# The second block of v columns in a gMLP layer: eight block products against seven, on one Trainium2 core

## The chip, the cores and the metric

The kernel runs on one core of one Trainium2 chip. The metric is the device time of one execution in microseconds (us). TensorE (PE) multiplies matrices, its weight loads are listed apart as PEld; VectorE (DVE) and ScalarE (ACT) do element-wise work, GpSimd (POOL) a few fills, and SyncE (SP) issues nearly all the transfers from memory.

## The reference, cut to what matters

The model is a trunk of two layers on 512 tokens of width 1024: attention, a dense SwiGLU, then a gMLP ("token mixing") and a second SwiGLU. Each sub-layer's output is normalised, gated and added to x, and x is normalised, scaled and shifted into the next sub-layer's input h. The change is in the gMLP:

```python
def token_mixing_mixer(h, w_in, ln_g, w_s, b_s, w_out):
    uv = jax.nn.gelu(h @ w_in)            # (512, 1024) @ (1024, 2048)
    u, v = jnp.split(uv, 2, axis=-1)      # 1024 columns each
    v = layer_norm(v, ln_g)               # over the 1024 columns of v
    ...                                   # chunks of 128 tokens, 8 groups of 128 columns
    sv = jnp.einsum('gts,bnsgc->bntgc', ws, v) + b_s.T[None, None, :, :, None]
    return (u * sv.reshape(B, S, D)) @ w_out
```

## The kernel before, in words

**Numbers in two parts.** Every operand of a matrix product is kept as a high and a low part in a reduced float32 (`F32R`). `split` writes the high part with ACT (a copy) and the low part with DVE (the difference). `mm3` then makes one product with three matmuls: high x high, high x low, low x high. A tile of 128x1024 numbers that comes from memory ("raw") therefore costs one ACT copy ("wh") and one DVE subtraction ("wl") before TensorE can use it.

**Weights.** `stream` is the list of all weight tiles in order of use. `wget(key, look)` hands out the next one and emits the loads and splits of up to `look` tiles beyond it. A raw tile lies in the pool `wraw`, which has two buffers; a split pair lies in `wpool` and `wpool2`, together six buffers. `s4` is a pool of 28 slots of 4 KB for everything else. Loads go through SP's queue in one order.

**Who sets the order.** The program is handed to a scheduler that fixes the order of instructions on each engine when the kernel is built, by program order and by its own estimate of when operands and buffers are there. Each engine then works its list from front to back and waits where something is late. In some stages the kernel chains the order by hand (`pe["chain"]`, `dve.chain`); not in the gMLP.

**The boundary in front of the gMLP.** `out_proj` ends the first SwiGLU; for each of four token tiles `tt` of 128 tokens, `boundary` normalises, adds to x, normalises again, has TensorE transpose the result ("tp") and splits it into `hT` (the input, features on the partitions). While the last two tiles pass through, three jobs fill TensorE: `v_first` twice (first 512 columns of v, token tiles 0 and 1) and `u_first` (the first 128 columns of u, tokens 0 to 255).

**The gMLP.** `gmlp` does, in order: the first 512 columns of v for token tiles 2 and 3 (48 matmuls of 128x512); the rest of u's first block (24 of 128x256); the second 512 columns of v for all four token tiles (96 of 128x512); gelu and `bn_stats`; then u's blocks 1 to 7 (`u_unit`), between which the normalised v is mixed (`mix`, "sv"). For v, the stationary operand is a 128x128 piece of `hT` and the moving one a row of 512 weight columns. Weight tiles of v are `("win_v", half, j)`, each with 256 of the 1024 input features, four for a half.

**In the background.** `bg.step(n)` advances the preparation of the next boundary's scale and shift ("A", "B"): each step loads 512 KB of modulation weights ("rawada") and adds a multiple of an earlier one to a sum on DVE (`scalar_tensor_tensor`, "B<-rawada,sc,B"). Its buffers are two.

**Seven products, elsewhere in this kernel.** Both SwiGLUs already compute a 2x2 block product by seven half-size products instead of eight (`Ffn.seven`): the weights are cut in four blocks B11, B12, B21, B22, of which sums T1 to T4 are made; of the activations the sums "1" to "4" are needed, which `boundary` makes with `sums` when it is given a dictionary `S`. For the first two token tiles it keeps an unsplit copy ("c"); for each of the other two, `sums` makes four DVE additions ("fs") and four splits ("Sh", "Sl"). At the boundary in front of the gMLP, `S` was None.

**Offsets.** `wtile` places a pair at an offset inside its buffer: 16 by default, `SHORT` (29 and 61 in turn) for the weights of matmuls that are 256 wide, 0 for the seven-product blocks of the last down projection.

Of the kernel before, what the change touches and what calls it, by code (L numbers as in the profile page):

```python
# [33 lines left out]
def trunk(ctx: ExitStack, tc: tile.TileContext, A: dict, out: bass.AP):  # L34
# [109 lines left out]
    def wload():  # L144

        src, a, b, key = stream[len(raws)]
        if src is None:
            raws.append(block_loads(key[1]))
            return
        raw = wraw.tile([P, a, b], F32, tag="raw", name=nm("raw"))  # L150
        load(raw[:], src)
        raws.append(raw)

    def wemit():
        n = len(got)
        src, a, b, key = stream[n]
        if len(raws) == n:
            wload()
        if src is None:
            if not first_blocks or n > first_blocks[-1] + KF:  # L160
                first_blocks.append(n)
            for _ in blocks(*next_raws(n)):
                pass
            return
        raw = raws[n]
        if key[0] == "wdn" and key[2] in SEVEN[key[1]]:
            got.append(down_blocks(raw))
            return
        h, l = wtile(a, b, SHORT if key[0] in ("wgu", "win_u") else 16)
        if key[0] == "wqk" and key[1]:  # L170

            act.activation(h[:], raw[:], AF.Copy)
            nc.vector.tensor_tensor(l[:], raw[:], h[:].bitcast(F32), ALU.subtract)
            if len(raws) == n + 1 and stream[n + 1][3][0] == "wqk":
                wload()
        else:
            high = act.activation(h[:], raw[:], AF.Copy)
            last_low[0] = nc.vector.tensor_tensor(l[:], raw[:], h[:].bitcast(F32), ALU.subtract)  # L178
# [17 lines left out]
    def block_loads(idx):  # L196

        x = wraw.tile([P, KD, P], F32, tag="raw", name=nm("rawx"))
        y = fwork["raw"].tile([P, KD, P], F32, tag="raw2", name=nm("rawy"))
        load(x[:], A["wx"][idx])
        load(y[:], A["wy"][idx])
        return x, y

    def next_raws(n):

# [115 lines left out]
    for l in range(2):  # L324
        for f in range(NH):
            wadd("wgu", 8, P, l, f, 0)
            wadd("wgu", 8, P, l, f, 1)
        for f in range(NH, KF):
            stream.append((None, 0, 0, ("blocks", (l, f - NH))))
        if l == 1:  # L330
            for q in range(2):
                for p in PAIRS[q]:
                    wadd("wdn", 4, 256, q, p)
        if l == 0:
            for f in range(KF):
                wadd("wdown", 1, D, f)
            for j in range(4):
                wadd("win_v", 2, 512, 0, j)
            wadd("win_u", 8, P, 0)
            for j in range(4):  # L340
                wadd("win_v", 2, 512, 1, j)
            for m in range(1, KD):
                wadd("win_u", 8, P, m)
            for k in range(KD):
                wadd("wout", 1, D, k)
# [1105 lines left out]
        return lambda: [v_gelu(v0["b"], tt, 0) for tt in range(2) if 3 in js]  # L1451

    def u_first(hT):
        v0["u"] = wget(("win_u", 0), 1)
        return u_unit(hT, 0, 0, 256, v0["u"])

    def gmlp(bg, hT, nhT, nS, nxt):
# [5 lines left out]
        u_unit(hT, 0, 256, 256, v0["u"])()  # L1463
        for tt in (2, 3):
            v_gelu(vb, tt, 0)
        vb = [bank("v") for _ in range(NT)]
        for k in range(4):
            if k % 2 == 0:
                wv = wget(("win_v", 1, k // 2))
            for tt in range(NT):  # L1470
                v_mm(hT, vb, tt, k, wv)
            bg.step(STEPS)
        wsr = wraw.tile([P, KD, P], F32, tag="raw", name="wsr")
        load(wsr[:], A["ws"])
        nc.gpsimd.memset(wsr[0:64, :, 64:P], 0.0)
# [2 lines left out]
            split(w[:, :, 0:P], w[:, :, P:], wsr[:, 4 * i : 4 * i + 4, :])  # L1478
        bsb = slot(F32, "bsb", KD, P)
        load(bsb[:].rearrange("p a b -> p (a b)"), A["bs"].to_broadcast([P, D]))  # L1480
        tail = [wget(("win_v", 1, j)) for j in (2, 3)]
        st = small.tile([P, NT, 2, 6], F32, tag="bns", bufs=1, name=nm("bns"))
        mv = small.tile([P, NT, 2], F32, tag="mv", bufs=1, name=nm("mv"))
        for tt in range(NT):
            for k in range(4, KD):
                v_mm(hT, vb, tt, k, tail[k // 2 - 2])
            v_gelu(vb, tt, 1)
            for hf in range(2):
                dve.bn_stats(st[:, tt, hf, :], vt[tt][:, 0, hf * 512 : (hf + 1) * 512])
            dve.bn_aggr(mv[:, tt, :], st[:, tt, :, :])  # L1490
# [69 lines left out]


    hT1, hT2, hT3 = {}, {}, {}
    S1, S3 = {}, {}
# [5 lines left out]
    bg2 = Bg("A2", "B2", lag=1, gap=3)  # L1569
    f0.run(  # L1570
        Bg("G1", slots=1), Bg("A1", "B1", "G2", slots=3, lag=2, flat=True), bg2, 2, hT2,
        [lambda: v_first(hT2, (0, 1)), lambda: v_first(hT2, (2, 3)), lambda: u_first(hT2)],
    )
    gmlp(bg2, hT2, hT3, S3, f1.first())
    f1.last(Bg("G3", slots=1))
# [2 lines left out]
def _layout(i):  # L1578

    f = np.ascontiguousarray  # L1580

    def fout(w):
        m = w.shape[1] // P
        return w.reshape(KD, P, m, P).transpose(2, 1, 0, 3)

    def blocks(a, b):

        return (
            np.concatenate([a[:, :, :4], b[:, :, 4:]], 2),
            np.concatenate([a[:, :, 4:], b[:, :, :4]], 2),  # L1590
        )
# [12 lines left out]
    wqkv = i["sb_w_qkv"][0]  # L1604
    a["wqk"] = np.stack([fout(wqkv[:, :D]), fout(wqkv[:, D : 2 * D])], 1)
    a["wv"] = vhalf(wqkv[:, 2 * D :])
    a["wo"] = slabs(i["sb_w_o"][0])
    gu = [(fout(i["ffn_w_gate"][l]), fout(i["ffn_w_up"][l])) for l in range(2)]
    a["wgu"] = np.stack([np.stack([g[:3], u[:3]], 1) for g, u in gu])
    a["wx"], a["wy"] = [np.stack(t) for t in zip(*[blocks(g[3:], u[3:]) for g, u in gu])]  # L1610
    a["wdown"] = slabs(i["ffn_w_down"][0])

    w = i["ffn_w_down"][1].reshape(NF, 2, P, 2, 2, 256).transpose(4, 0, 2, 1, 3, 5)
    w = w.reshape(2, NF, P, 4, 256).copy()
    for q in range(2):
# [4 lines left out]
    a["win_v"] = vhalf(i["tm_w_in"][0][:, D:])  # L1620
    a["wout"] = slabs(i["tm_w_out"][0])
# [55 lines left out]
```

## Time and profile before

| | before |
|---|---|
| median of 3 runs | 1104.61 us (1103.84 to 1106.79) |
| span of the profiled execution | 1104.6 us, which is the time of the median run to the digits shown |
| PE busy | 1085.9 us (98%), 7404 matmuls |
| PEld busy | 979.0 us (89%) |
| DVE busy | 945.9 us (86%) |
| ACT busy | 594.2 us (54%) |
| second half of v on TensorE | 649.81 to 671.59 us, 96 matmuls |
| u's blocks 1 to 4 on TensorE, behind it | 671.59 to 693.92 us, 192 matmuls |

A matmul's time in the list is longer than the step from one matmul to the next, since matmuls overlap in the array; what counts is the step, that is the difference of two starts. Times in the timeline are microseconds from the span's start.

### The profile page before, as it was taken

The page shows a single profiled execution, that of the slowest core. Times are in us where ns is not written, and L with a number is a line of the kernel's source. Part 1 is how long each engine was busy: PE and PEld are TensorE (multiplying, and loading weights), DVE is VectorE, ACT ScalarE, POOL GpSimd, SP SyncE. Part 2 cuts the span into 40 slices and gives each one's busy share as a digit, 9 for nine tenths or more (in the row PEclk, how much of TensorE's full clock was granted, in tenths as well). Part 3 has the DMA queues.
Part 4 walks back from the last instruction along what each step waited for, and adds up shares of the span by engine and source line. Part 5 has one row for each costly group of instructions (what it writes and reads, how often), then busy time and mean ns, then how long its engine had stood idle before and what let it go on. Part 6 is the DMA issues. An engine that isn't in the chain of part 4 may idle for free.

```text
span 1104.6 us, 18512 instructions
## 1 busy us (share of the span) xinstructions
PE 1085.9 (98%) x7404; PEld 979.0 (89%) x7404; DVE 945.9 (86%) x1248; ACT 594.2 (54%) x982; POOL 29.5 (3%) x53
## 2 busy tenths in 40 slices
PE   6999999999999999999999999999999999999997
PEld 4787788788999999998888889988999999989996
DVE  4988999966989999989866967668979999899997
ACT  6554665665655555554243626426555555565662
POOL 0020100000000000000000000001000000000000
PEclk9999999999999999999999999999999999999999
DMA  8976434304433434359757465334334343333252
GB/s 302 370 226 217 142 116 133 125 11 152 157 112 131 162 119 146 132 197 351 272 191 256 144 205 196 96 116 155 128 117 155 128 159 102 110 115 96 77 187 81
DMA packets 51355, 176.38 MB, mean 160 GB/s; under 512 B 6074, under 2 KB 9146, under 8 KB 51268
## 3 DMA queue, kind: packets, MB, share of 16 engines
q1 hardware_dynamic: 48708, 166.81, 44.6%
q0 software_dynamic: 2560, 8.39, 2.1%
q8 instruction: 58, 0.95, 0.3%
q14 instruction: 29, 0.24, 0.1%
HBM read 164.69 MB, written 8.39 MB: 157 GB/s over the span
## 4 chain that ended last, share of the span: by engine, by line
PE 90%; DVE 4%; DMA 2%; ACT 2%; issue 1%; SPq 0%; DVEq 0%; ACTq 0%
PE r L109 32%; PE y L109 18%; PE pqk L109 7%; PE gu L109 6%; PE v L109 5%; PE X L109 4%; PE u L109 4%; PE Y L109 3%; PE av L109 2%; PE z L109 2%; PE tw L117 1%; PE tp L117 1%; PE Z L109 1%; PE W L109 1%; PE ab L109 1%
## 5 line engine op out<-in xcount | busy, mean ns | idle before, releaser
L87 ACT ACTIVATE wh<-raw 128x1024 fp32r<-128x1024 f32 (+1 forms) x112 | 115.7, 1038 | 130.5 <-PE y L109 39.4
L109 PE MATMUL r<-Sh,wh 128*128 128x256 f32 x608 | 168.1, 276 | 0.5 <-ACT e L87 0.5
L109 PE MATMUL r<-Sh,wl 128*128 128x256 f32 x608 | 167.9, 276 | 0.0
L109 PE MATMUL r<-Sl,wh 128*128 128x256 f32 x608 | 167.9, 276 | 0.0
L109 PE MATMUL y<-wh,as 128*128 128x512 f32 x480 | 149.9, 390 | 0.0
L178 DVE TENSOR_TENSOR wl<-raw,wh 128x1024 fp32r<-128x1024 f32 x87 | 105.8, 1222 | 48.2 <-ACT wh L87 47.6
L109 PEld LDWEIGHTS r<-Sh,wh 128*128 128x128 f32 x608 | 114.1, 188 | 1.0 <-ACT e L87 0.9
L109 PEld LDWEIGHTS r<-Sl,wh 128*128 128x128 f32 x608 | 114.1, 188 | 0.1
L109 PEld LDWEIGHTS r<-Sh,wl 128*128 128x128 f32 x608 | 114.1, 188 | 0.0
L109 PEld LDWEIGHTS y<-wh,as 128*128 128x128 f32 x480 | 90.0, 188 | 18.6
L71 DVE TENSOR_TENSOR wl<-f,wh 128x1024 fp32r<-128x1024 f32 x87 | 103.2, 1220 | 0.0
L87 ACT ACTIVATE wh<-f 128x1024 fp32r<-128x1024 f32 x87 | 91.8, 1055 | 15.3 <-DVE f L71 11.6
L87 ACT ACTIVATE e<-r 128x256 f32<-128x256 f32 x114 | 43.7, 385 | 101.8 <-PE r L109 100.8
L109 PE MATMUL y<-wl,as 128*128 128x512 f32 x240 | 93.7, 391 | 0.0
L109 PE MATMUL r<-hTh,wh 128*128 128x256 f32 x304 | 84.2, 277 | 0.2 <-DVE gu L71 0.2
L109 PE MATMUL r<-hTl,wh 128*128 128x256 f32 x304 | 84.0, 276 | 0.0
L109 PE MATMUL r<-hTh,wl 128*128 128x256 f32 x304 | 84.0, 276 | 0.0
L109 PE MATMUL r<-hTh,b 128*128 128x256 f32 x304 | 57.9, 276 | 0.0
L109 PEld LDWEIGHTS r<-hTh,wh 128*128 128x128 f32 x304 | 57.1, 188 | 0.9 <-DVE gu L71 0.9
L109 PEld LDWEIGHTS r<-hTh,wl 128*128 128x128 f32 x304 | 57.1, 188 | 0.0
L109 PEld LDWEIGHTS r<-hTl,wh 128*128 128x128 f32 x304 | 57.1, 188 | 0.0
L87 ACT ACTIVATE wh<-rawx 128x1024 fp32r<-128x1024 f32 x38 | 40.4, 1063 | 29.8 <-PE r L109 29.0
(262 smaller groups left out, 2937.1 us busy)
## 6 DMA issues: line engine op xcount, KB each, us to landing
rawada<-in_ada SPq DMA_DIRECT2D x80, 512.0 KB, 5.7
rawy<-in_wy SPq DMA_DIRECT2D x38, 512.0 KB, 4.6
rawx<-in_wx SPq DMA_DIRECT2D x38, 512.0 KB, 3.7
raw<-in_wdown SPq DMA_DIRECT2D x22, 512.0 KB, 5.4
raw<-in_wdn SPq DMA_DIRECT2D x22, 512.0 KB, 3.6
raw<-in_wqk SPq DMA_DIRECT2D x16, 512.0 KB, 3.9
ada<-in_ada0p SPq DMA_DIRECT2D x12, 512.0 KB, 6.3
raw<-in_wgu SPq DMA_DIRECT2D x12, 512.0 KB, 3.5
```

Of the source, the lines that this page charges most:

```text
L71: b = getattr(nc.vector, op)(*args, **kw)
L87: b = nc.scalar.activation(*args, **kw)
L109: b = nc.tensor.matmul(o, l, r, start=start, stop=stop, skip_group_check=True)
L117: last_tp[0] = nc.tensor.transpose(o, i, ident)
L178: last_low[0] = nc.vector.tensor_tensor(l[:], raw[:], h[:].bitcast(F32), ALU.subtract)
```

## The change

The second 512 columns of v are computed as a 2x2 block product by seven products instead of eight. The blocks are two halves of the tokens (256), two halves of the input features (512) and two halves of the columns (256). `boundary` is given `S2`, so that it makes the activation sums; the weights come as four blocks of 512 features x 256 columns (`vblock_loads`), two in `wraw` and two in `s4` slots, and `vblocks` splits them and makes and splits the sums T1 to T4, one step for each product. Each product is 24 matmuls of 128x256 (two token tiles, four feature tiles, three parts), in the order A11, 1, 2, 4, 3, A12, A22, with three PSUM banks R1 to R3. Partial results are copied out by ACT (`s1`, `s5`, `u1`) and put together by DVE before gelu (`out_v`). Each product is followed by one background step (seven in all); before, each of the first four feature tiles of this part was followed by two (eight in all). `u_first` no longer looks ahead by one weight tile.

```diff
+    def vblock_loads():
+        r = [wraw.tile([P, 4, 256], F32, tag="raw", name=nm("raw")) for _ in range(2)]
+        r += [slot(F32, "rawv", 4, 256) for _ in range(2)]
+        r = dict(zip(("B11", "B21", "B12", "B22"), r))
+        for n, t in r.items():
+            load(t[:], A["wvs"]["B11 B12 B21 B22".split().index(n)])
+        return r
+
+    def vblocks(r):
+        def ready(src):
+            h, l = wtile(4, 256, SHORT)
+            split(h, l, src)
+            return h, l
+        def total(a, b, tag="f13"):
+            ...
+            dve.tensor_tensor(f[:], a[:], b[:], ALU.add)
+            return f
+        yield ready(r["B11"][:])
+        t1 = total(r["B11"], r["B12"])
+        yield ready(t1[:])
+        t2 = total(t1, r["B22"], "f24")
+        yield ready(t2[:])
+        yield ready(r["B22"][:])
+        t3 = total(r["B22"], r["B12"])
+        yield ready(t3[:])
+        yield ready(r["B21"][:])
+        t4 = total(t2, r["B21"])
+        yield ready(t4[:])
...
-            for j in range(4):
-                wadd("win_v", 2, 512, 1, j)
+            stream.append((None, 0, 0, ("vblocks",)))
...
     def u_first(hT):
-        v0["u"] = wget(("win_u", 0), 1)
+        v0["u"] = wget(("win_u", 0), 0)
...
-        vb = [bank("v") for _ in range(NT)]
-        for k in range(4):
-            if k % 2 == 0:
-                wv = wget(("win_v", 1, k // 2))
-            for tt in range(NT):
-                v_mm(hT, vb, tt, k, wv)
-            bg.step(STEPS)
+        W = wget(("vblocks",), 0)
+        R1, R2, R3 = [bank(n)[:].rearrange("p (s c) -> p s c", s=2) for n in ("r1", "r2", "r3")]
+        def product(o, a, start, stop):
+            wh, wl = next(W)
+            for s in range(2):
+                for k in range(4):
+                    ...
+                    mm3(
+                        o[:, s], h, l, wh[:, k, :], wl[:, k, :],
+                        start and s + k == 0, stop and k == 3,
+                    )
+            bg.step(1)
...
+        product(R1, "A11", True, False)
+        act.activation(s1, R1, AF.Copy)
+        product(R3, "1", True, False)
+        act.activation(s5, R3, AF.Copy)
+        product(R1, "2", False, False)
+        act.activation(u1, R1, AF.Copy)
+        product(R3, "4", False, True)
+        for s in range(2):
+            out_v(s, 1, R3[:, s], u1[:, s], ALU.subtract)
+        product(R1, "3", False, False)
+        for s in range(2):
+            out_v(2 + s, 1, s5[:, s], R1[:, s], ALU.subtract)
+        product(R2, "A12", True, True)
+        for s in range(2):
+            out_v(s, 0, R2[:, s], s1[:, s], ALU.add)
+        product(R1, "A22", False, True)
+        for s in range(2):
+            out_v(2 + s, 0, R1[:, s])
...
-        tail = [wget(("win_v", 1, j)) for j in (2, 3)]
...
-            for k in range(4, KD):
-                v_mm(hT, vb, tt, k, tail[k // 2 - 2])
-            v_gelu(vb, tt, 1)
...
-        [lambda: v_first(hT2, (0, 1)), lambda: v_first(hT2, (2, 3)), lambda: u_first(hT2)],
+        [lambda: v_first(hT2, (0, 1)), lambda: v_first(hT2, (2, 3)), lambda: u_first(hT2)], S2,
```

More of the change, by code (lines that the diff above doesn't have):

```diff
@@ L147, in wload @@
         if src is None:
-            raws.append(block_loads(key[1]))
+            raws.append(block_loads(key[1]) if key[0] == "blocks" else vblock_loads())
             return
@@ L158, in wemit @@
             wload()
+        if key[0] == "vblocks":
+            got.append(vblocks(raws[n]))
+            return
         if src is None:
@@ L205, in block_loads @@
         return x, y
+    def vblock_loads():
[11 more added lines that the diff above has]
+        def total(a, b, tag="f13"):
+            f = fwork["pool"].tile(
+                [P, 4, 256], F32, tag=tag, name=nm("f"), **({"bufs": 1} if tag == "f24" else {})
+            )
[12 more added lines that the diff above has]
+        yield ready(t4[:])
     def next_raws(n):
@@ L1465, in gmlp, with out_v @@
             v_gelu(vb, tt, 0)
-        vb = [bank("v") for _ in range(NT)]
-        for k in range(4):
-            if k % 2 == 0:
-                wv = wget(("win_v", 1, k // 2))
-            for tt in range(NT):
-                v_mm(hT, vb, tt, k, wv)
-            bg.step(STEPS)
+        W = wget(("vblocks",), 0)
[4 more added lines that the diff above has]
+                for k in range(4):
+                    if a in "1234":
+                        h, l = [t[:, k, s * P : (s + 1) * P] for t in S2[a]]
+                    else:
+                        at = 256 * (a[1] == "2") + s * P
+                        h, l = hB(hT, k + 4 * (a[2] == "2"), at, P)
+                    mm3(
+                        o[:, s], h, l, wh[:, k, :], wl[:, k, :],
+                        start and s + k == 0, stop and k == 3,
+                    )
+            bg.step(1)
+        su = slot(F32, "su")
+        s1, u1 = [su[:, i, :].rearrange("p (s c) -> p s c", s=2) for i in range(2)]
+        s5 = slot(F32, "s5")[:, 0, :].rearrange("p (s c) -> p s c", s=2)
+        def out_v(tt, c, *sum2):
+            o = vt[tt][:, 0, 512 + c * 256 : 768 + c * 256]
+            if len(sum2) > 1:
+                dve.tensor_tensor(o, *sum2)
+            last_act[0] = act.activation(o, o if len(sum2) > 1 else sum2[0], AF.Gelu_apprx_tanh)
+        product(R1, "A11", True, False)
[16 more added lines that the diff above has]
+            out_v(2 + s, 0, R1[:, s])
         wsr = wraw.tile([P, KD, P], F32, tag="raw", name="wsr")
@@ L1562, in trunk @@
     hT1, hT2, hT3 = {}, {}, {}
-    S1, S3 = {}, {}
+    S1, S2, S3 = {}, {}, {}
     f0, f1 = Ffn(1, 0, hT1, S1), Ffn(3, 1, hT3, S3)
@@ L1620, in _layout @@
     a["win_v"] = vhalf(i["tm_w_in"][0][:, D:])
+    a["wvs"] = i["tm_w_in"][0][:, D + 512 :].reshape(2, 4, P, 2, 256).transpose(0, 3, 2, 1, 4).reshape(4, P, 4, 256)
     a["wout"] = slabs(i["tm_w_out"][0])
```

## The prediction

> **What bounds the kernel now.** I read the page's busy shares first, then the chain that ended last around the gMLP, then the busy time by stage.
>
> ```profile
> PE 1085.9 (98%) x7404; PEld 979.0 (89%) x7404; DVE 945.9 (86%) x1248; ACT 594.2 (54%) x982; POOL 29.5 (3%) x53
> ...
> PE 90%; DVE 4%; DMA 2%; ACT 2%; issue 1%; SPq 0%; DVEq 0%; ACTq 0%
> ```
> ```profile
> 636.17 10.90 PE v L109 x48
> 647.07 2.74 PE u L109 x24
> 649.81 21.78 PE v L109 x96
> 671.59 22.33 PE u L109 x192
> ```
> ```profile
> core 0: us, PE busy (x) PEld busy (x) DVE busy (x) ACT busy (x) POOL busy (x), PEclk, DMA share, GB/s
> 636.00:650.00 14.00, 14.00 (x76) 12.06 (x75) 8.43 (x9) 4.76 (x6) 0.00 (x0) 1.00 0.50 177
> 650.00:672.00 22.00, 22.00 (x101) 18.28 (x100) 14.20 (x17) 6.74 (x10) 0.52 (x1) 1.00 0.83 278
> 672.00:694.00 22.00, 22.00 (x192) 22.00 (x191) 16.51 (x19) 15.83 (x19) 0.00 (x0) 1.00 0.45 139
> ```
>
> The chain runs through TensorE for 90% of the span, and its pieces from 636.17 to 693.92 follow each other without a gap, at the full granted clock (1.00). So in this stage TensorE's list is the time: a matmul saved is time saved, as long as the list never waits. DVE is the next engine: 22.6 of the 36 us from 636 to 672, so 13.4 us idle.
>
> **The change, part by part.** All terms are set against the profiled span of 1104.6 us, which is also the median of the three runs (1104.61).
>
> *TensorE, removed and added.* The 96 matmuls of 128x512 took 21.78 us, 227 ns a step. In their place come 7 x 24 = 168 matmuls 256 columns wide. Two rows price that width. The u piece above has steps of 2.74 / 24 = 114 ns; there the weights are stationary and the tokens move. In the last down projection's seven products the roles are those of the changed code (activations stationary, weight blocks moving):
>
> ```profile
> 994.00 0.28 PE L109 MATMUL Z<-wh,ah 128*128 128x256 f32 x1
> ...
> 998.94 0.39 PE L109 MATMUL X<-wh,ah 128*128 128x512 f32 x1
> ```
>
> Between these starts lie 42 matmuls of 128x256: 4.94 / 42 = 117.6 ns. So 168 cost 19.1 us at the first price and 19.8 at the second, and the saving is 2.7 or 2.0 us. I take 2.0, because the roles are the same; but those blocks lie at offset 0 and the new ones at 29 or 61, like the weights of the u piece, so 2.7 stays as the other end. More than 2.7 us, 0.25% of the kernel, can't be had from this edit: no other stage loses work.
>
> [...]
>
> *The activation sums.* These rows price them: the groups over the whole program, and the timeline of the later boundary, where DVE makes the same sums among other work.
>
> ```profile
> L87 ACT ACTIVATE Sh<-fs x16: 610/633/635, 299.4 to 794.8; 128x512 fp32r<-128x512 f32 x16
> L71 DVE TENSOR_TENSOR Sl<-fs,Sh x16: 682/684/693, 300.1 to 799.4; 128x512 fp32r<-128x512 f32 x16
> L71 DVE TENSOR_TENSOR fs<-fs,c x8: 684/685/686, 298.7 to 794.1; 128x512 f32<-128x512 f32 x8
> L87 ACT ACTIVATE c<-tp x8: 577/598/601, 267.7 to 762.6; 128x512 f32<-128x512 f32 x8
> ```
> ```profile
> 778.31 0.68 DVE L71 TENSOR_TENSOR fs<-c,tp 128x512 f32<-128x512 f32 x1
> ...
> 779.24 1.28 DVE L71 TENSOR_TENSOR hTl<-tp,hTh 128x512 fp32r<-128x512 f32 x2
> ...
> 799.38 0.68 DVE L71 TENSOR_TENSOR Sl<-fs,Sh 128x512 fp32r<-128x512 f32 x1
> 800.64 2.36 DVE L71 TENSOR_TENSOR wl<-f,wh 128x1024 fp32r<-128x1024 f32 x2
> ```
>
> Two token tiles x (4 additions + 4 low parts) x 0.685 = 11.0 us of DVE; 8 high parts x 0.633 and 4 copies "c" x 0.598 = 7.5 us of ACT. ACT is idle for 24.5 of the 36 us, and the copies of tiles 0 and 1 fall into the boundary, where TensorE has the other tiles' matmuls; I cost ACT at nothing. If that cover were gone, a copy costs 0.6 us.
>
> *The weights.* Seven splits in place of four, and four sums. One low part is 1.22 us, but two in a row take 2.36 (row above), so about 1.16 each: 7 x 1.16 = 8.1 us against 4.6, and 4.6 for T1 to T4.
>
> *Putting together.* Six DVE operations of 128x256 in place of none, at 0.42 us as in this row of the SwiGLU, and three ACT copies and eight small gelus in place of four large ones:
>
> ```profile
> 803.40 0.42 DVE L71 TENSOR_TENSOR gu<-r,e 128x256 f32<-128x256 f32 x1
> ```
>
> That is 2.5 us of DVE. No TensorE wait follows from it: R1 and R3 are read while the next product fills another bank, 2.8 us for a copy of under 0.7.
>
> *Does DVE keep up?* Added are 11.0 + 3.5 + 4.6 + 2.5 = 21.6 us, where 13.4 were idle, and the stage gets 2 us shorter. So the cover is gone on average, and it is the order that decides.
>
> ```profile
> 633.97 2.19 PE u L109 x19
> ```
> ```profile
> 634.20 1.29 DVE L71 TENSOR_TENSOR hTl<-tp,hTh 128x512 fp32r<-128x512 f32 x2 [1.00 <-ACT hTh L87]
> 640.04 1.23 DVE L178 TENSOR_TENSOR wl<-raw,wh 128x1024 fp32r<-128x1024 f32 x1 [3.95 <-ACT wh L87]
> 641.18 2.60 DVE L71 SCALAR_TENSOR_TENSOR B<-rawada,sc,B 128x1024 f32<-128x1024 f32 x2
> 657.32 1.28 DVE L71 SCALAR_TENSOR_TENSOR B<-rawada,sc,B 128x1024 f32<-128x1024 f32 x1 [2.69 <-DMA rawada<-in_ada]
> 662.47 1.28 DVE L71 SCALAR_TENSOR_TENSOR B<-rawada,sc,B 128x1024 f32<-128x1024 f32 x1 [0.16 <-DMA rawada<-in_ada]
> ...
> 751.79 1.28 DVE L71 SCALAR_TENSOR_TENSOR t<-t,r,B 128x1024 f32<-128x1024 f32 x1
> ```
>
> The last token tile is transposed by 633.97, and the first product starts at 649.81. Product "1", the first to need sums, follows at 652.6, 18.6 us after the transposes. By then DVE owes the two "hTl" (1.3), the sums (11.0), B11, T1 and its sum (3.5) and the two "B" (2.6): 18.4, just in time, with no bubble allowed. It can begin earlier than 634, because the low part of the v tile that `u_first` looked ahead to (1.2 us) no longer stands there. By the start of the last product, 649.81 + 6 x 2.82 = 666.7, it owes in addition the rest of the weights (12.7 - 3.5 = 9.2), six more "B" that stand in front of later weights in the program (7.7) and four combinations (1.7): 37.0 us in 32.7, or some 34 if operations overlap by 0.07 as the pair above does. `bn_stats`, `ws` and u's low parts are behind these and can slip past. So DVE comes out level or a few us late at the last two products. The boundary that uses "B" comes at 751.79, so the scheduler may push it back and the lateness is nought; the other end is rival 2. I take 0.6 us of waiting.
>
> *Transfers and queues.* The bytes are the same: four loads of 512 KB. Two of them now need `s4` slots, beside ten more slots for the sums and copies. B11 takes the place in SP's queue of the load that u's first tile used to look ahead to:
>
> ```profile
> 625.51 6.15 SPq L126 DMA_DIRECT2D raw<-in_win_v  x3
> ...
> 644.95 0.33 SPq L126 DMA_DIRECT2D raw<-in_win_u  x1
> ```
> ```profile
> raw<-in_win_u SPq DMA_DIRECT2D x8, 512.0 KB, 5.8
> ```
> ```profile
> 650.79 1.06 ACT L87 ACTIVATE wh<-raw 128x1024 fp32r<-128x1024 f32 x1 [3.08 <-DMA raw<-in_win_u]
> ```
>
> What moves back is u's block 1. It was loaded at 644.95, 26.6 us ahead of its matmuls; now its raw buffer is the one that B21 leaves, after T4's sum. Issued at 660, it lands at 665.8 (5.8, the median in the row above), is split by 668.1 (1.06 and 1.22), and TensorE wants it at 649.81 + 19.8 = 669.6: in time by 1.5 us. Issued at 666 it would be 4.5 us late. I put the wait at nothing, since T4's sum needs only the buffer that T1's leaves, which is free once T1 is split, before 652.6.
>
> *Behind the stage.* Gelu and `bn_stats` end in a smaller tail (two gelus of 256 in place of one of 512), and 22 us of u's matmuls lie before the first "sv": free.
>
> *Sum.* 1104.6 - 2.0 + 0.6 = 1103.2 us.
>
> **The rivals.**
>
> 1. *The low price, and no wait.* 168 x 114 ns, DVE level: 1104.6 - 2.7 = 1101.9. For it speaks the offset; against it the roles.
>
> 2. *DVE's list stands behind "B" (slower).* The scheduler fixes DVE's order; where a "B" whose transfer is late stands in front of a weight's low part, TensorE waits too. The trace shows one such wait of 2.69 us, harmless because weights were far ahead. Each wait in front of products 2 to 7 costs that much; one cancels the saving (1105.3), three give 1104.6 - 2.0 + 8.1 = 1110.7. It is slower by over 0.3% from two waits on, also through a late u block 1. Against it: the weight buffers of the first half of v come free one by one before 647, so that T1 to T3 can be split before the products begin.
>
> 3. *The width does not pay.* If a 256-wide matmul took as long as its weight load in the list does, step would not follow width:
>
> ```profile
> L109 PEld LDWEIGHTS r<-Sh,wh 128*128 128x128 f32 x608 | 114.1, 188 | 1.0 <-ACT e L87 0.9
> ```
> 168 x 188 ns = 31.6 us, so 1104.6 + 9.8 = 1114.4. Against it: the u matmuls have the same load each and step at 114. [...]
>
> 4. *Saved here, given back.* Waits on DVE and on u's block 1 add up to the saving: 1104.6.
>
> **How the numbers follow.** The forecast holds 0.54, rival 1 0.20, rival 2 0.12, rival 3 0.02, rival 4 0.12. I call 0.3% (3.3 us) what a measurement can tell, since the three runs spread over 2.95 us. Only rival 1 with a lucky spread is below 1101.3: 0.08 faster. Rivals 2 and 3 give 0.14 slower; the rest, 0.78, is the same. The range goes from 1101.4 (rival 1 less half a microsecond of spread) to 1107.1 (the forecast's saving with u's block 1 late by 4.5 us), which leaves out about 2 in 10. I predict 1103.2 us.
>
> **What would show it.** Right: 168 matmuls "r" of 128x256 in place of 96 "v", steps of 114 to 118 ns, TensorE without a gap from the u piece to u's block 1, which starts about 2 us sooner after 649.8. Wrong: TensorE waiting for "wl" or "Sl" of DVE at a product, a "B" with a transfer's wait just in front of that low part, or u's block 1 waiting for its raw tile; a step under 114 would make the saving larger than I allow.

## The result and the profile after

The changed kernel takes 1114.97 us (median of 5 runs, 1113.54 to 1116.84) against 1106.11 us for the kernel before (5 runs, 1103.84 to 1107.18): ratio 1.0083, 95% interval 1.007 to 1.0096. It is slower, by some 9 us, and outside the range that was forecast. The profiled execution took 1113.54 us, with a span of 1111.8. One of the eleven executions of a later kernel, spaced, took 2796.74 us: its ratio leaves that one out, and since it was the profiled one, a profile of its neighbour spaced_off0 is read in its place.

The page's shares and the chain's shares by engine, of the kernel after:

```profile
PE 1086.0 (98%) x7476; PEld 982.4 (88%) x7476; DVE 964.7 (87%) x1277; ACT 605.9 (54%) x1004; POOL 29.6 (3%) x53
...
PE 87%; DVE 6%; DMA 4%; ACT 2%; issue 1%; SPq 0%; DVEq 0%; ACTq 0%
```

TensorE has 72 more matmuls (168 in place of 96) and as much busy time as before, but the chain runs through it for 87% of the span in place of 90%: the rest went to DVE and transfers, that is to waits. What TensorE waited for between 640 and 720 us (total, times, longest); the same view of the kernel before has no row there:

```profile
PE adaps L109 <- DVE A L71: 3.0, 1, 3.0
PE u L109 <- DVE wl L181: 3.0, 1, 3.0
PE r L109 <- DVE wl L71: 1.3, 1, 1.3
```

TensorE's timeline of the kernel after: the first product, and the three waits.

```profile
648.46 0.28 PE L109 MATMUL r<-wh,hTh 128*128 128x256 f32 x1
...
651.34 0.40 PE L109 MATMUL adaps<-acch,ones 128*128 128x512 f32 x1
...
653.68 0.39 PE L109 MATMUL r<-wl,Sh 128*128 128x256 f32 x1 [1.30 <-DVE wl L71]
...
674.93 0.39 PE L109 MATMUL u<-hTh,wl 128*128 128x256 f32 x1 [2.99 <-DVE wl L181]
...
711.42 0.50 PE L109 MATMUL adaps<-acch,ones 128*128 128x512 f32 x1 [2.99 <-DVE A L71]
```

The 24 matmuls of product A11 fill 648.46 to 651.34, a step of 120 ns. At that price 168 take 20.2 us against 21.78 before: the change saves 1.6 us where it was meant to. Then it waits 1.30 + 2.99 + 2.99 = 7.3 us in three places, of which only the first lies in the products. SP's queue shows how each came about:

```profile
644.67 0.33 SPq L126 DMA_DIRECT2D rawada<-in_ada  x1
645.09 0.86 SPq L126 DMA_DIRECT2D rawv<-in_wvs  x2
...
664.72 0.33 SPq L126 DMA_DIRECT2D raw<-in_win_u  x1
...
693.10 13.16 SPq L126 DMA_DIRECT2D raw<-in_wout  x5
706.31 0.42 SPq L126 DMA_DIRECT2D g<-in_pre_g  x1
```

So does DVE's timeline of the same kernel:

```profile
643.36 1.28 DVE L71 SCALAR_TENSOR_TENSOR B<-rawada,sc,B 128x1024 f32<-128x1024 f32 x1
...
649.62 1.23 DVE L71 TENSOR_TENSOR f<-raw,rawv 128x1024 f32<-128x1024 f32 x1 [0.21 <-DMA rawv<-in_wvs]
651.27 1.23 DVE L71 TENSOR_TENSOR f<-f,rawv 128x1024 f32<-128x1024 f32 x1 [0.42 <-DMA rawv<-in_wvs]
652.41 1.22 DVE L71 TENSOR_TENSOR wl<-f,wh 128x1024 fp32r<-128x1024 f32 x1
...
663.47 1.22 DVE L71 TENSOR_TENSOR wl<-raw,wh 128x1024 fp32r<-128x1024 f32 x1
...
669.70 1.28 DVE L71 TENSOR_TENSOR ws<-wsr,ws 128x512 fp32r<-128x512 f32 x2
670.90 1.45 DVE L71 BATCH_NORM_STATS2 bns<-vt 128x6 f32<-128x512 f32 x2
...
673.70 1.17 DVE L181 TENSOR_TENSOR wl<-raw,wh 128x1024 fp32r<-128x1024 f32 x1
...
710.68 0.69 DVE L71 SCALAR_TENSOR_TENSOR A<-adaps,g 128x512 f32<-128x512 f32 x1 [0.47 <-DMA g<-in_pre_g]
```

1. *Product "1".* B12 and B22 ("rawv", 645.09) stand in SP's queue right behind a "rawada" load, which goes out at 644.67, just as the "B" of 643.36 frees its buffer. They land some 5 us later, and DVE, which waits for each of them (0.21 and 0.42 us), makes both sums and only then T1's low part, which ends at 653.6; TensorE wanted it at 652.4.
2. *u's block 1.* Its raw buffer comes free when B21's low part ends (663.47 + 1.22 = 664.69); the load goes out at 664.72. ACT splits it at 669.11 (below), but DVE has "ws" and the whole of "bn_stats" ahead of its low part, which starts at 673.70. TensorE wanted u's block 1 at 671.9.
3. *The preparation of A.* "A<-adaps,g" multiplies by the row "g" (`pre_g`). Before, "g" was loaded at 645.33; it now stands behind five loads of "wout" in the queue and goes out at 706.31. The next "adaps" matmul waits for this "A", and stops TensorE, in whose list it stands.

Two more views give the price of the rest: ACT's timeline, and the busy time by stretch (columns as in the prediction).

```profile
669.11 1.06 ACT L87 ACTIVATE wh<-raw 128x1024 fp32r<-128x1024 f32 x1 [1.88 <-DMA raw<-in_win_u]
```
```profile
649.00:672.00 23.00, 21.61 (x170) 20.52 (x169) 22.16 (x26) 13.14 (x22) 0.52 (x1) 1.00 0.71 245
675.00:680.00 5.00, 5.00 (x30) 5.00 (x31) 3.95 (x7) 4.12 (x6) 0.00 (x0) 0.66 0.51 150
680.00:685.00 5.00, 5.00 (x46) 5.00 (x45) 5.00 (x6) 4.97 (x6) 0.00 (x0) 1.00 0.17 65
```

DVE is busy for 22.16 of 23 us in the products. And behind the second wait the granted clock is 0.66 for 5 us: 30 matmuls where the next 5 us have 46, a loss of 0.34 x 5 = 1.7 us.

The spans of the two profiled executions differ by 7.2 us (1111.8 against 1104.6), but part of that has nothing to do with the stage: the first matmul of the program into a tile "v" starts at 23.72 us before and at 22.15 after. So the stage is compared by itself, from the last matmul of u's first block to the first transpose ("tp") of the next boundary. It takes 103.6 us before (649.53 to 753.13) and 111.8 after (648.34 to 760.18), 8.2 us more. The waits above count only from the end of the matmul in front of them, which the profile models. From start to start, less a step, they cost 7.9 us (652.00 to 653.68, 671.66 to 674.93, 708.16 to 711.42). The balance is -1.6 + 7.9 + 1.7 = +8.0 us.

### The profile page after: what moved, and what is told of

Same layout as the page of the kernel before. It is cut to its first block, busy times and chain, and to the rows that moved or that the text cites. A ratio compares the mean times of both kernels' runs of the same rounds, so it can differ in the third digit from the quotient of the medians.

```text
span 1111.8 us, 18704 instructions
## 1 busy us (share of the span) xinstructions
PE 1086.0 (98%) x7476; PEld 982.4 (88%) x7476; DVE 964.7 (87%) x1277; ACT 605.9 (54%) x1004; POOL 29.6 (3%) x53
## 4 chain that ended last, share of the span: by engine, by line
PE 87%; DVE 6%; DMA 4%; ACT 2%; issue 1%; SPq 0%; DVEq 0%; ACTq 0%
PE r L109 33%; PE y L109 17%; PE pqk L109 7%; PE gu L109 6%; PE X L109 4%; PE v L109 4%; PE Y L109 3%; PE av L109 2%; PE z L109 2%; PE tw L117 1%; PE Z L109 1%; PE W L109 1%; PE tp L117 1%; PE u L109 1%; PE ab L109 1%
## 5 line engine op out<-in xcount | busy, mean ns | idle before, releaser
L87 ACT ACTIVATE wh<-raw 128x1024 fp32r<-128x1024 f32 (+1 forms) x110 | 113.4, 1036 | 118.1 <-PE y L109 39.0
L181 DVE TENSOR_TENSOR wl<-raw,wh 128x1024 fp32r<-128x1024 f32 x83 | 100.8, 1221 | 44.2 <-ACT wh L87 43.6
L109 PEld LDWEIGHTS r<-Sh,wh 128*128 128x128 f32 x608 | 114.1, 188 | 1.1 <-ACT e L87 1.0
L109 PEld LDWEIGHTS r<-Sl,wh 128*128 128x128 f32 x608 | 114.1, 188 | 0.1
L109 PEld LDWEIGHTS r<-Sh,wl 128*128 128x128 f32 x608 | 114.1, 188 | 0.0
L71 DVE TENSOR_TENSOR wl<-f,wh 128x1024 fp32r<-128x1024 f32 x91 | 108.1, 1221 | 0.0
L87 ACT ACTIVATE wh<-f 128x1024 fp32r<-128x1024 f32 x91 | 96.0, 1055 | 14.1 <-DVE f L71 5.9
```

The lines of the kernel that those rows point to most:

```text
L71: b = getattr(nc.vector, op)(*args, **kw)
L87: b = nc.scalar.activation(*args, **kw)
L109: b = nc.tensor.matmul(o, l, r, start=start, stop=stop, skip_group_check=True)
```

## The experiments

Two theories were set against each other. **Theory 1, order:** the products save what their step says, and the loss is lists and queues in a bad order (SP's queue, the two raw buffers, the fixed lists of DVE and TensorE); with the order mended the loss goes, though the work stays. **Theory 2, work:** DVE simply has too much to do, and any order is late somewhere. The kernel before ran beside each; the table gives all comparisons.

| kernel | ratio to before | 95% interval | what TensorE still waits for, 640 to 725 us | at half clock, us | stage, us |
|---|---|---|---|---|---|
| before | | | none | 0 | 103.6 |
| after | 1.0083 | 1.007 to 1.0096 | 1.3 + 3.0 + 3.0 | 3.4 | 111.8 |
| one_more_step | 1.0085 | 1.0065 to 1.0105 | 1.8 + 2.8 + 2.7 | 6.8 | 114.1 |
| early_loads | 1.0078 | 1.006 to 1.0097 | 2.5 + 0.6 + 1.6 + 2.1 | 6.8 | 111.8 |
| u_ahead | 1.0072 | 1.0058 to 1.0087 | 1.0 + 0.5 + 3.0 | 3.4 | 109.0 |
| all_three | 1.0028 | 1.0018 to 1.0038 | 0.9 + 1.0 + 1.8 | 3.4 | 107.6 |
| sums_alone | 1.0015 | 1.0004 to 1.0026 | 0.4 + 2.2 | 0 | 106.5 |
| no_sums | 1.0029 | 1.0019 to 1.0039 | 0.3 + 2.6 | 3.4 | 106.5 |
| no_bg | 1.0017 | 1.0003 to 1.003 | none; 0.9 to 1.3 three times before 640 | 3.4, before the stage | 102.0 |
| pool_t | 1.0061 | 1.0048 to 1.0074 | 5.1 | 6.8 | 109.9 |
| spaced | 0.9997 | 0.9988 to 1.0006 | (not read) | (not read) | (not read) |
| spaced_off0 | 0.9998 | 0.9989 to 1.0007 | 0.8 | 0 | 102.4 |
| spaced_off16 | one run, 1104.57 us | | 0.5 | 0 | 102.5 |
| gap4 | 1.0013 | 1.0004 to 1.0023 | 2.4 | 3.4, at 97 us | 103.9 |

The last three columns are of one execution each, the profiled one. "At half clock" is the time at a granted clock of 0.50, without the last 5 us of the span (there the kernel before is at 0.50 from 1102.00, the kernel after from 1108.93); "stage" is the stretch defined above. In every row the stage differs from that of the kernel before by the saving of the products (1.6 us; 2.1 at offset 0; none in sums_alone), the waits, and half of the time in which TensorE worked at half clock, to within 0.9 us (1.3 in one_more_step). So the waits and the clock are the loss; the question is what makes TensorE wait.

### One mending at a time

*one_more_step*: the eighth background step back, so that "g" is asked for early.

```diff
         product(R1, "A22", False, True)
+        bg.step(1)
```

> The changed kernel with one background step more, behind the last product (eight in all, as before the change). Theory 1, order of SP's queue: the row of gains "g" for A is again asked for in the v stage instead of behind five tiles of wout, so the 3.0 us that TensorE waited for A's scaled row at its adaps matmul go, the waits of 1.3 and 3.0 us at product "1" and at u's block 1 stay: 3 us less than the changed kernel, ratio to before near 1.0055. Theory 2, too much DVE work: DVE is full from 649 to 672, so the work that is moved forward shows up as a later wait: within 1 us of the changed kernel, ratio 1.007 to 1.009.

SP's queue and TensorE's timeline of this run:

```profile
660.77 0.33 SPq L126 DMA_DIRECT2D g<-in_pre_g  x1
```
```profile
656.38 0.39 PE L109 MATMUL r<-wl,Sh 128*128 128x256 f32 x1 [1.80 <-DVE wl L71]
...
679.01 0.38 PE L109 MATMUL u<-hTh,wl 128*128 128x256 f32 x1 [2.83 <-DVE wl L181]
...
715.31 0.76 PE L109 MATMUL adaps<-accl,ones 128*128 128x512 f32 x1 [2.74 <-DVE accl L71]
```

The load of "g" went out 45 us earlier, and the third wait stayed, now for DVE's "accl": 1115.86 us, no gain. The late load was only what came last. Behind it stood DVE's chain from A to B, late for another reason. The clock also fell twice here, behind the first wait and behind the third, to 0.50 for 6.8 us in all. The expectation of order missed; the ratio is in the range of the other theory.

*early_loads*: the four blocks loaded in the boundary in front, as soon as buffers allow. *u_ahead*: u's blocks 1 and 2 asked for ahead of "wsr" (the raw tile of "ws").

```diff
     def u_first(hT):
         v0["u"] = wget(("win_u", 0), 0)
+        wload()
```
```diff
             out_v(2 + s, 0, R1[:, s])
+        for _ in range(2):
+            wemit()
         wsr = wraw.tile([P, KD, P], F32, tag="raw", name="wsr")
```

> The changed kernel with the four block loads issued right behind u's first tile, ahead of the background's loads in SP's queue. Theory 1: B12 and B22 land before 640 instead of 650, T1 and T2 are made in time, and the 1.3 us wait at product "1" goes; DVE also catches up by some of its idle time before 649, so u's block 1 may wait less: 1.3 to 3 us less than the changed kernel, ratio near 1.006. Theory 2: T1 can't be split any sooner since DVE is busy with the activation sums until 645: nothing changes, ratio 1.008.

> The changed kernel with the load and split of u's blocks 1 and 2 asked for ahead of the mixing weights ws, so that they take the raw buffers first and stand ahead of ws and bn_stats on DVE. Theory 1: u's block 1 is there at the end of the products, the wait of 3.0 us goes, and with it the granted clock of 0.66 behind it (some 1.5 us): 4 to 4.5 us less than the changed kernel, ratio near 1.004. Theory 2: DVE is full, so u's block 1 is late by about as much: 0 to 1 us less.

TensorE's timeline of early_loads, then of u_ahead:

```profile
673.47 0.39 PE L109 MATMUL u<-hTh,wh 128*128 128x256 f32 x1 [2.53 <-ACT wh L87]
```
```profile
654.74 0.39 PE L109 MATMUL r<-wl,Sh 128*128 128x256 f32 x1 [1.05 <-DVE wl L71]
...
706.03 0.50 PE L109 MATMUL adaps<-acch,ones 128*128 128x512 f32 x1 [2.95 <-DVE A L71]
```

With the blocks early, product "1" no longer waits, and the wait turns up at u's block 1, 2.53 us. With u ahead, u's block 1 is on time, and product "1" and "adaps" wait as they did; the fall of the clock (to 0.50 for 3.4 us) has moved behind "adaps". Each mending takes away its own wait, and not the next one. By their ratios the two runs lie where theory 2 had them, or next to it; the waits that went are those that theory 1 named.

*all_three*: the three edits together.

> The three edits together (early block loads, u's blocks ahead of ws, the eighth background step). Theory 1: no wait of TensorE is left in the stage, and what remains is the saving of the products, 168 x 120 ns = 20.2 us against 21.8: 1 to 2 us faster than before, ratio 0.9985 to 0.999. Theory 2: waits of several us remain at the last products or at u's block 1, because DVE's sums and splits don't fit: ratio 1.002 to 1.006.

1108.72 us, ratio 1.0028: products (168 in 20.2 us) and u's blocks 1 to 4 run without a gap. That is a ratio from the range of theory 2, without the waits that it named. What is left is the chain of "A" and "B". TensorE's timeline, and one row of ACT's:

```profile
702.12 0.50 PE L109 MATMUL adaps<-accl,ones 128*128 128x512 f32 x1 [0.93 <-DVE accl L71]
...
704.23 0.51 PE L109 MATMUL adaps<-acch,ones 128*128 128x512 f32 x1 [1.02 <-ACT acch L87]
...
707.88 0.50 PE L109 MATMUL adaps<-accl,ones 128*128 128x512 f32 x1 [1.77 <-DVE accl L71]
```
```profile
696.38 1.06 ACT L87 ACTIVATE wh<-raw 128x1024 fp32r<-128x1024 f32 x1 [2.48 <-DMA raw<-in_wout]
```

Three waits, 3.7 us, for small operations of the next boundary's scale and shift. That boundary uses "B" tens of us later (its first "t<-t,r,B" was at 751.79 before); the "adaps" matmuls that finish it, though, stand among u's and "sv"'s in one list. A DVE without time is not what holds "accl" and "acch" up at this place: from 694 to 720 us DVE is busy for 18.88 of 26 us (row further below). They stand in DVE's and ACT's lists behind the splits of wout's tiles, and ACT waits for those tiles, as in the row above. The first of these loads goes out 21.8 us behind the start of u's block 1 (692.83 and 671.04); in the kernel before it was 12.3 us (683.74 and 671.43).

### Which work makes the chain late

*sums_alone*: the kernel before, which also makes the activation sums and doesn't use them. *no_sums*: the changed kernel without them; products "1" to "4" read plain blocks of `hT`, so v is another one.

```diff
-    S1, S3 = {}, {}
+    S1, S2, S3 = {}, {}, {}
...
-        [lambda: v_first(hT2, (0, 1)), lambda: v_first(hT2, (2, 3)), lambda: u_first(hT2)],
+        [lambda: v_first(hT2, (0, 1)), lambda: v_first(hT2, (2, 3)), lambda: u_first(hT2)], S2,
```
```diff
-                        h, l = [t[:, k, s * P : (s + 1) * P] for t in S2[a]]
+                        h, l = hB(hT, k, 256 * (a in "24") + s * P, P)
...
-        [lambda: ..., lambda: ..., lambda: u_first(hT2)], S2,
+        [lambda: ..., lambda: ..., lambda: u_first(hT2)],
```

> The kernel before, in which the boundary also makes the activation sums and the copies for them; v is computed as before and nothing reads the sums. It prices 11 us of DVE and 7.5 us of ACT by themselves. If the sums fit into DVE's idle time of 13.4 us (636 to 672), as my prediction had it, the time is that of before within 0.15%. If they are what the stage can't carry, TensorE waits behind it, at u's block 1 or at the adaps matmuls, and the ratio is 1.002 to 1.005.

> The changed kernel without the activation sums: products 1 to 4 read plain blocks of the input in their place, so the output is another; the matmuls, the weights' sums and splits and all loads stay. Theory 2 (too much DVE work): with 11 us of DVE gone, most of the 7.3 us of waits go, ratio 1.000 to 1.002. Theory 1 (order of SP's queue and of the raw buffers): u's block 1 still waits for the buffer that B21 holds and the weight tiles behind it stay late, ratio 1.004 to 1.007.

TensorE's timeline of sums_alone, then of no_sums:

```profile
703.03 0.50 PE L109 MATMUL adaps<-acch,ones 128*128 128x512 f32 x1 [2.21 <-ACT acch L87]
```
```profile
703.79 0.65 PE L109 MATMUL adaps<-acch,ones 128*128 128x512 f32 x1 [2.58 <-ACT acch L87]
```

In sums_alone v runs as before (96 matmuls in 21.79 us), and the sums cost 0.15%. In the profile TensorE waits only at "adaps", more than 50 us after the sums were made. Without the sums the changed kernel has its other waits short or gone, the chain is still late by 2.6 us, and the clock falls behind it (0.72 from 703.80 to 709.80); the ratio lies between the ranges of the two theories. So either half of the added work is enough to make the chain late in the order that the lists have. That it is DVE's share of this work is not shown: the sums also bring 7.5 us to ACT, and in sums_alone, just before the wait, ACT stood idle for 2.59 us (until 695.01) and DVE for 2.03 (until 696.10) because a wout tile had not landed.

*no_bg*: all_three, with seven of the eight accumulations of the last part of "B" left out, so that this B is another one.

```diff
-                        ada_stt(ada[group[i // KD][:2]], raws[i], i % KD)
+                        if group[i // KD][0] != "B" or group[i // KD][1] != 2 or i % KD == 0:
+                            ada_stt(ada[group[i // KD][:2]], raws[i], i % KD)
```

> The kernel with the three edits, without seven of the eight accumulations of the background's B on DVE (its loads stay; the next boundary's shift comes out as another number). It takes 9 us of DVE work out between 636 and 672. Theory 2: DVE is level again, low parts of u and wout come earlier, the waits of 3.7 us at the adaps matmuls go, and the ratio is 0.997 to 0.9985. Theory 1: wout's loads still start at 693 because the raw buffers come free late, the waits stay, ratio 1.002 to 1.003.

What TensorE waited for in no_bg from 605 to 650 us, one row of its DVE timeline and two of SP's queue:

```profile
PE tp L117 <- DVE t L71: 2.3, 2, 1.3
PE u L109 <- DVE wl L181: 0.9, 1, 0.9
```
```profile
620.38 1.29 DVE L71 SCALAR_TENSOR_TENSOR x<-t,r,x 128x1024 f32<-128x1024 f32 x1 [2.44 <-DMA x<-xd]
```
```profile
602.11 11.80 SPq L126 DMA_DIRECT2D rawada<-in_ada  x4
613.95 0.98 SPq L126 DMA_DIRECT2D x<-xd  x2
```

Seven operations of DVE less, 7.1 us of its busy time (956.3 against 963.4), and the "adaps" waits are gone; yet its interval overlaps that of all_three. With fewer operations the scheduler made another order: the load of x now stands behind "rawada" loads and goes out at 613.95 (600.46 in all_three). DVE waits 2.44 us for it, TensorE waits three times in the boundary in front, 3.2 us in all, and behind that the clock is at half until 640.48. The stage itself is 1.6 us shorter than before, which is the saving of the products. So with less work the stage has no wait left, as theory 2 said, and the new order loses the gain in front of it; the ratio it named, 0.997 to 0.9985, was not met.

*pool_t*: all_three, with the four weight sums on GpSimd.

```diff
-            dve.tensor_tensor(f[:], a[:], b[:], ALU.add)
+            nc.gpsimd.tensor_tensor(f[:], a[:], b[:], ALU.add)
```

> The kernel with the three edits, with the four weight sums T1 to T4 made by GpSimd, which is idle, in place of DVE: 4.9 us off DVE. Theory 2: the waits at the adaps matmuls shrink by 2 to 4 us, ratio 0.999 to 1.001. Theory 1: no change, 1.003. If GpSimd takes over 4 us for one sum, T2 comes late and a wait at product "2" takes their place: 1.004 or more.

GpSimd's timeline, then DVE's and TensorE's:

```profile
635.35 2.89 POOL L230 TENSOR_TENSOR f<-rawv,rawv 128x1024 f32<-128x1024 f32 x1
```
```profile
636.46 2.33 DVE L71 TENSOR_TENSOR Sl<-fs,Sh 128x512 fp32r<-128x512 f32 x1
```
```profile
670.78 0.58 PE L109 MATMUL r<-wh,hTh 128*128 128x256 f32 x1 [5.07 <-DVE vt L71]
```

Slower than all_three, 1112.98 us, with four sums taken off DVE. An addition costs 2.6 to 2.9 us on GpSimd against 1.23 on DVE. That alone is not what TensorE waits for, though: product A22 waits 5.07 us for the "vt" that reads product "3" out of the bank R1, and in the new list that "vt" stands behind five "B" and u's low parts. The clock is at half for 6.8 us around the end of this wait: a step is 0.21 us until 676.28 and 0.12 behind that. Nor did DVE gain time: while GpSimd added, a "Sl" took 2.33 us on DVE that takes 0.68 elsewhere, and DVE's busy time is 965.2 us in place of 963.4. So pool_t says nothing on what less work for DVE would do; it has fewer operations on DVE, none of its time back, and a worse order.

### The order alone

*spaced*: all_three, with three background steps behind each of u's blocks 4 to 7 in place of five, so that the pairs of "adaps" stand apart by one u block each.

```diff
                 mixed(m - 4)
-                bg.step(5)
+                bg.step(3)
```

> The kernel with the three edits and three background steps behind each of u's blocks 4 to 7 in place of five, so that the four adaps pairs of A and B come one to a block and not two inside block 5. If the 3.7 us of waits that were left are only this chain put too early into TensorE's list while DVE is behind, they go, the granted clock stays at 1.00, and what is left is the shorter product time (20.2 against 21.8 us): 0.998 to 1.000 of before. If DVE is too full whatever the order, adaps or the mixing waits elsewhere and the ratio stays at 1.002 to 1.003.

*spaced_off0* and *spaced_off16* are spaced with the weight blocks at another offset in their buffers:

```diff
-            h, l = wtile(4, 256, SHORT)
+            h, l = wtile(4, 256)
```
```diff
-            h, l = wtile(4, 256, SHORT)
+            h, l = wtile(4, 256, 16)
```

> The same with the split weight blocks at offset 0 of their buffers in place of 29 and 61. My forecast took 117.6 ns from matmuls of the same roles at offset 0; the changed kernel steps at 120.4. If the offset makes the difference, the products step at 117.6 here: 19.8 us for 168, 0.5 us less than spaced (under what the timing can tell). If not, 120.4 stays.

> The same at offset 16, the one of the v weights before. One look at the step: 117.6, 120.4 or, as for the u weights, 114 ns.

spaced is at 0.9997, spaced_off0 at 0.9998 of before: 0.3% better than all_three, by one digit in the source. Read in the profile of spaced_off0, the page's shares and the stretch from 694 to 720 us stand behind those of all_three:

```profile
PE 1086.0 (98%) x7476; PEld 982.2 (89%) x7476; DVE 963.4 (87%) x1277; ACT 605.2 (55%) x1004; POOL 29.6 (3%) x53
```
```profile
694.00:720.00 26.00, 22.28 (x166) 21.30 (x165) 18.88 (x29) 11.21 (x16) 0.00 (x0) 0.93 0.44 139
```
```profile
PE 1082.2 (98%) x7476; PEld 980.5 (89%) x7476; DVE 963.3 (87%) x1277; ACT 605.4 (55%) x1004; POOL 29.5 (3%) x53
```
```profile
694.00:720.00 26.00, 25.17 (x188) 23.66 (x187) 25.07 (x45) 13.80 (x19) 0.00 (x0) 1.00 0.51 166
```

DVE does the same 1277 operations in 963.4 and 963.3 us. But in this stretch TensorE is busy for 25.17 us in place of 22.28, at the full clock in place of 0.93: of the three waits of 3.7 us one of 0.8 is left. DVE is busier there (25.07 us in place of 18.88), and TensorE waits less. Here the work is equal and only the order differs; that settles it between the theories for these 3 us.

The step of a product differed with the offset in these runs. TensorE's timeline of spaced_off0, first product and first u behind the last one:

```profile
647.23 0.28 PE L109 MATMUL r<-wh,hTh 128*128 128x256 f32 x1
...
666.93 0.28 PE L109 MATMUL u<-hTh,wh 128*128 128x256 f32 x1
```

168 in 19.70 us: 117.3 ns. In spaced_off16, whose lists for TensorE, DVE and ACT are the same operation for operation, it is 120.0 (20.16 us); in all_three, at 29 and 61, 120.4 (20.23 us). The 0.5 us between offset 0 and 29 and 61 can't be seen in the medians of spaced_off0 and spaced (1105.68 and 1105.65).

*gap4*: spaced_off0, with one more step between the split of a piece of A or B and the "adaps" that read it.

```diff
-    bg2 = Bg("A2", "B2", lag=1, gap=3)
+    bg2 = Bg("A2", "B2", lag=1, gap=4)
```

> The spaced kernel at offset 0 with one step more between the split of a piece of A or B and its adaps matmul (gap 4 in place of 3), so that each adaps pair stands a whole u block behind its split. If the 0.5 to 0.8 us wait at the second adaps pair was the last that the order left, TensorE has no gap from the products to wout, and the gMLP is 2.1 us (21.8 against 19.7) shorter than before: 0.998 to 0.999, with an interval that may still touch 1. If the last pieces of A and B now come too late, a wait shows at the last mixing blocks, and the ratio is 1.000 or more.

TensorE's timeline of gap4:

```profile
719.97 0.50 PE L109 MATMUL adaps<-acch,ones 128*128 128x512 f32 x1 [2.38 <-ACT acch L87]
```

1107.98 us, 0.13% slower than before. Now the first three pairs wait for nothing, and the last one, pushed back among "wout"'s first matmuls, waits 2.38 us. The chain can stand too early in TensorE's list and too late; both cost the same kind of wait. Its price in the stage is small: 103.9 us, 0.3 more than before. The profiled execution, the slowest of twelve (1109.53 us), lost more elsewhere: TensorE waited 1.91 us at 96.50 and worked at half clock from 97.15 to 100.57 (mean clock of the execution 0.997, 0.998 in spaced_off0), in a part where the lists of gap4 and spaced_off0 are the same. How much of the 0.13% is the edit's stays open.

## Why the prediction was wrong, by its steps

The forecast was 1104.6 - 2.0 + 0.6 us. In its terms the stage came out at -1.6 for the products, +7.9 for waits where 0.6 stood, and +1.7 for the clock, for which there was no term.

**TensorE, removed and added: right in kind, too large.** Product for product the saving is there. The term was 2.0 us at 117.6 ns; the blocks at offsets 29 and 61 take 120.4 ns (all_three), so 1.6 us. 117.6 is the step of offset 0, as spaced_off0 shows with 117.3. The prediction saw that the offsets differ and took it to speak for a *lower* step.

**Step and width, rival 3.** The width paid. The steps were 117 to 120 ns at 256 columns (117.3 in spaced_off0, 120.4 in all_three) against 227 at 512, and in every version whose products run without a wait the products take 19.7 to 20.2 us against 21.78. The kernel is slower, but not from that.

**Does DVE keep up?: the sum was near, the wait mis-sized.** 21.6 us were to be added; over the program DVE's busy time grew by 18.8 (964.7 against 945.9). It said that DVE would come out level or a few us late and that order would decide; DVE is busy for 22.16 of 23 us. The 0.6 us of waiting was the mis-sized term: product "1" alone waited 1.30, and not because DVE was full, but because B12 and B22 landed late. With them fell the argument against rival 2, that T1 to T3 could be split before the products begin: T1's low part started at 652.41.

**"The boundary that uses "B" comes at 751.79, so the scheduler may push it back and the lateness is nought": the step that failed most quietly.** It looked at who uses B, and not at what stands behind the matmuls that finish B. Those stand in TensorE's own list among u's matmuls, so a late A stops TensorE some 40 us before the boundary wants it: 3.0 us in the kernel after, 3.7 in all_three, 2.6 in sums_alone.

**Transfers and queues: the step that failed as it said it might.** u's block 1 was put at no wait for an issue at 660 us, and at 4.5 us late for one at 666. It went out at 664.72, 5 us after what the sum assumed: the prediction took the raw buffer of B21 to be free early "since T4's sum needs only the buffer that T1's leaves", but B21's own low part on DVE was what held it, to 664.69. And the low part of u's block stood behind "ws" and "bn_stats", which the text let "slip past". The order of SP's queue was read for one load (B11); the loads that now stood behind "rawada" and behind "wout", the second pair of blocks and "g", were not followed.

**Behind the stage: not free.** Besides the waits, a granted clock of 0.66 over 5 us cost 1.7 us, a term that the sum didn't have. Gelu and "bn_stats" were put at nothing there, and the low part of u's block 1 stood behind them.

**The rivals.** Rival 2 had the sign, and its mechanism in part: an in-order list with something late in front of a low part. It counted on 2.69 us for each wait and 1110.7 us at most. What came was three waits, one in the products, one at u's block 1 and one it didn't have, and the clock. Rival 1's step of 114 ns was not met by any version; rival 4, all saved and given back, has the time of spaced, though the profile of spaced_off0 shows only 0.8 us given back.

**What stays open.** The profiled execution of spaced_off0 was the fastest of its eleven (1102.72 us; the others 1104.24 to 1107.03). Part of that is its start: its first "v" matmul stands at 21.42 us, that of the kernel before at 23.72. From there to the end of the span it is 1.3 us shorter (1079.6 against 1080.9), about what its products save less its wait. The medians of spaced and spaced_off0 show only 0.1 to 0.2 us of it, and their intervals reach from 1.2 or 1.3 us saved to 0.7 or 0.8 lost; whether the other executions lose the saving was not seen. Why the wout loads start later behind a changed stage was not tested by itself. Why no_bg's list came out as it did is the scheduler's estimate, which no trace shows.

## What to carry to other kernels

Where one engine is the bound and works a fixed list, the saving in a stage is the small, certain term; what decides is each item in that list whose inputs come through an engine or a queue that the change fills up or puts in another order, however late the result itself is needed. So follow, for each queue that the change touches, what now stands behind a load whose buffer isn't free, and for each nearly full engine, which waits of the bound's list hang on its order. Test with an edit that changes only the order at equal work: it shows at once whether to take work away or to move it.

## What the runs showed of the hardware

**The granted clock fell behind some waits, and not behind others.** It was 0.66 from 675.00 to 680.00, behind the wait of 2.99 us at 674.93. Cut more finely, four stretches of the kernel after (columns as in the prediction), around that wait and around the one of 2.99 us at 711.42:

```profile
672.02:675.44 3.42, 0.51 (x4) 0.51 (x5) 3.42 (x9) 1.01 (x3) 0.00 (x0) 1.00 0.54 183
675.44:678.85 3.41, 3.41 (x18) 3.41 (x18) 2.36 (x5) 3.10 (x5) 0.00 (x0) 0.50 0.48 154
706.16:709.57 3.41, 2.27 (x21) 2.08 (x19) 2.71 (x5) 2.07 (x3) 0.00 (x0) 1.00 0.79 267
709.57:712.98 3.41, 1.55 (x12) 1.51 (x13) 2.94 (x7) 0.00 (x0) 0.00 (x0) 1.00 0.57 195
```

The clock is at 0.50 for 3.41 us (675.44 to 678.85), a loss of 1.7 us. A step of u's matmuls is 0.21 us there and 0.12 us from 679.04 on. In no_sums the granted clock was 0.72 over the 6 us behind the wait of 2.58 us at 703.79. After the wait of 2.99 us at 711.42 in the kernel after (706.16 to 712.98), and of 2.21 us at 703.03 in sums_alone (703.00 to 709.00), it stayed at 1.00. In the kernel after, two waits of the same length thus came out differently; what tells them apart was not shown, and no run set out to test it.

**Beside GpSimd's additions three DVE operations took 1.71 to 2.33 us in place of 0.68.** In pool_t GpSimd added from 632.73 to 641.06 and from 644.20 to 646.92. In these times one "fs" took 1.71 us on DVE and two "Sl" 2.30 and 2.33; all three are 128x512, at 0.68 us elsewhere.

**The products' step differed with the offset of their weight blocks, the moving operand.** 117.3 ns at offset 0 (spaced_off0), 120.0 at 16 (spaced_off16), 120.4 at 29 and 61 (all_three), all 128x256 in fp32r with activations stationary.
